# A macaron transformer block: 24 of 38 activation tiles are transposed by VectorE in 32x32 blocks and rearranged through HBM

## The chip, the cores and the metric

The kernel runs on one core of a Trainium2 chip. The metric is the device time of one execution in microseconds (us), the median of several runs. A core has five engines that each work through their own queue in order and wait for one another by semaphores: TensorE (PE in the profile, PEld for its weight loads), VectorE (DVE), ScalarE (ACT), GpSimd (POOL) and SyncE (SP). The last three here also issue DMA transfers. Tiles lie in SBUF, 128 partitions wide; TensorE writes to PSUM.

## The reference

All in float32: 256 tokens, width 2048, one block.

```python
h = rms_norm(x, ffn1_norm[i])
x = x + 0.5 * swiglu_ffn(h, ffn1_w_gate[i], ffn1_w_up[i], ffn1_w_down[i])   # D_FF = 5632
h = rms_norm(x, mix_norm[i])
proj = h @ w_in[i]
...
y_a = s5_mixer(u_a, ...)          # a state-space scan, then a GLU of 1024 x 1024
y_b = sgu_mixer(uv_b, ...)        # a gated mixing of tokens
gates = jax.nn.sigmoid(h @ w_gate[i] + b_gate[i])
g_a, g_b = jnp.split(gates, 2, axis=-1)
merged = g_a * (y_a @ w_branch_a[i]) + g_b * (y_b @ w_branch_b[i])
x = x + merged @ w_out[i]
h = rms_norm(x, ffn2_norm[i])
x = x + 0.5 * swiglu_ffn(h, ffn2_w_gate[i], ffn2_w_up[i], ffn2_w_down[i])
...
return rms_norm(x, final_norm)
```

where `swiglu_ffn(h, g, u, d)` is `(silu(h @ g) * (h @ u)) @ d`.

## The kernel before

**Weights.** All weight matrices stream from HBM once, in chunks of 128x2048 floats (1 MB), in the order of use. SP loads a chunk into `raw`; `split_piece` (L148, L149) makes of it a rounded high part `whi` on ScalarE and the remainder `wlo` on VectorE. Each product is then three matmuls (L216 to L218): high by high, high by low, low by high.

**Steps.** `take` hands out a chunk in four pieces of 512 columns, and every piece is a *step*: six matmuls, three for each half of the tokens. At the start of a step `tick` runs, in this order: the hooks that are due, the evacuation of the job that just ended (`pend`), at every fourth step the split of the chunk two ahead of the one in use (three buffers of `whi` and `wlo`), and a slice of side work when there is credit for it. What `tick` emits stands in that order in each engine's queue, so the program's text sets the order of everything.

**Jobs.** A `job` is one output tile of 256 tokens x 512 columns: `kt` steps into one PSUM accumulator `acc` (three buffers), then its evacuation. `at(n, fn)` puts `fn` into the hooks of the step that is n later.

**Transposes.** TensorE contracts over partitions, so a result that is the next product's input has to be transposed. `turned` does so 2 steps after the evacuation: eight 128x128 transposes on TensorE (L258) into two PSUM tiles `q`, then `put`, which splits `q` into high and low part on ScalarE and VectorE (`split2`: L244, L245; `split_gain` with a norm's gain: L248, L249). There are 38 such tiles:

- the feed-forward blocks, 11 each: the gated hidden tile, in groups of 4, 4 and 3 (`GROUPS`). `gate_evac` (L319) applies silu, `up_evac` (L329) multiplies, and `put` writes to `gt`. After a group come four jobs of the down product;
- *the first residual*, 4: after the first block's last down product (jobs of 12 steps) `residual` adds to `x_sb` (L294), squares for the norm, and the columns of `x_sb` are transposed into the next `h`;
- the mixers, 4;
- *the merge*, 4: `ba_evac` (L1026, L1027, jobs of 8 steps) combines the two branches, into `mT`;
- *the residual after w_out*, 4: the same `residual`, jobs of 16 steps.

**Side work.** In the first feed-forward block `s5_prepare` computes the scan's tables, 0.3 to 0.35 slices a step, with transfers through HBM that GpSimd issues (`stash_e`, `stash_v`, `stash_c`, `stash_g`, `stash_t`, `stash_w`; `eb`, `bt`, `par`, `tt` are loads). Five slices lie between the load of `eb` and `bt` and their use.

Of the kernel before, what the change touches and what calls it, by code (L numbers as in the profile page):

```python
# [9 lines left out]
F32 = mybir.dt.float32  # L10
F32R = mybir.dt.float32r
BF16 = mybir.dt.bfloat16
AF = mybir.ActivationFunctionType
ALU = mybir.AluOpType
# [4 lines left out]
P = 128  # L19
D = 2048  # L20
T = 256
DFF = 5632
KD = D // P
KF = DFF // P
EPS = 1e-6
N = 512
# [19 lines left out]
def f(ap):  # L46
    return ap.bitcast(F32)
# [3 lines left out]
def kernel(  # L51
# [31 lines left out]
    act, dve, pe, pool = nc.scalar, nc.vector, nc.tensor, nc.gpsimd  # L83

    cst = ctx.enter_context(tc.tile_pool(name="cst", bufs=1))
    ev = ctx.enter_context(tc.tile_pool(name="ev", bufs=1))
    wp = ctx.enter_context(tc.tile_pool(name="wp", bufs=1))
    hp = ctx.enter_context(tc.tile_pool(name="hp", bufs=1))
    dr = ctx.enter_context(tc.tile_pool(name="dr", bufs=1, space=DRAM))
# [4 lines left out]
    x_sb = cst.tile([P, 2, D], F32, name="x_sb")  # L94
# [72 lines left out]
    def at(delta, fn):  # L167
        hooks.setdefault(st["tick"] + delta, []).append(fn)
# [40 lines left out]
    def new_acc():  # L209
        return ps.tile([P, 2, N], F32, tag="acc", name="acc")  # L210

    def step(acc, lhs, k, first, last):
        hi, lo = take(N)
        for h in range(2):
            t = slice(h * P, h * P + P)
            pe.matmul(acc[:, h, :], lhsT=lhs[:, k, 0, t], rhs=hi, start=first, stop=False)  # L216
            pe.matmul(acc[:, h, :], lhsT=lhs[:, k, 0, t], rhs=lo, start=False, stop=False)  # L217
            pe.matmul(acc[:, h, :], lhsT=lhs[:, k, 1, t], rhs=hi, start=False, stop=last)  # L218

    def job(lhs, kt, evac):  # L220
        acc = new_acc()
        for k in range(kt):
            step(acc, lhs, k, k == 0, k == kt - 1)
        pend.append(lambda: evac(acc))
# [12 lines left out]
    def tmp():  # L237
        return ev.tile([P, 2, N], F32, tag="t", name="t", bufs=2)
# [1 line left out]
    def small():  # L240
        return ev.tile([P, 8], F32, tag="sm", name="sm", bufs=2)

    def split2(dst, src):
        act.activation(out=dst[:, :, 0, :], in_=src, func=AF.Copy)  # L244
        dve.tensor_tensor(out=dst[:, :, 1, :], in0=src, in1=f(dst[:, :, 0, :]), op=ALU.subtract)  # L245

    def split_gain(dst, src, g, k):
        act.activation(out=dst[:, 0, :], in_=src, func=AF.Copy, scale=g[:, k:k + 1])  # L248
        dve.scalar_tensor_tensor(out=dst[:, 1, :], in0=src, scalar=g[:, k:k + 1],  # L249
                                 in1=f(dst[:, 0, :]), op0=ALU.mult, op1=ALU.subtract)  # L250

    def turned(src, c0, put):
        for b in range(2):
            q = ms.tile([P, 2, T], F32, tag="ms", name="q")
            for i in range(2):
                for h in range(2):
                    c = c0 + (2 * b + i) * P
                    pe.transpose(q[:, i, h * P:h * P + P], src[:, h, c:c + P], ident)  # L258
            put(b, q)

    def rsqrt(dst, q, n, scratch):
        act.activation(out=dst, in_=q, func=AF.Sqrt, scale=1.0 / n, bias=eps_t)
        dve.reciprocal(dst, dst)
        dve.scalar_tensor_tensor(out=scratch, in0=q, scalar=EPS * n, in1=dst,
                                 op0=ALU.add, op1=ALU.mult)
        dve.scalar_tensor_tensor(out=scratch, in0=scratch, scalar=-0.5 / n, in1=dst,
                                 op0=ALU.mult, op1=ALU.mult)
        dve.scalar_tensor_tensor(out=dst, in0=scratch, scalar=1.5, in1=dst,
                                 op0=ALU.add, op1=ALU.mult)

    def square(m, h):
        j = ev.tile([P, N], BF16, tag="junk", name="junk", bufs=1)
        act.activation(out=j, in_=x_sb[:, h, m * N:m * N + N], func=AF.Square,  # L273
                       accum_out=ssq[:, h, m:m + 1])
# [14 lines left out]
    def rc(h):  # L289
        return norm["r"][:, h:h + 1]  # L290

    def add_residual(acc, m, scale):
        xs = x_sb[:, :, m * N:m * N + N]
        dve.scalar_tensor_tensor(out=xs, in0=acc, scalar=scale, in1=xs, op0=ALU.mult, op1=ALU.add)  # L294

    def residual(hT, g, scale):
        def make(m):
            def put(b, q):
                for i in range(2):
                    k = 4 * m + 2 * b + i  # L300
                    split_gain(hT[:, k], q[:, i, :], g, k)

            def evac(acc):
                add_residual(acc, m, scale)
                for h in range(2):
                    square(m, h)
                at(2, lambda: turned(x_sb, m * N, put))
                if m == 3:
                    at(4, new_norm)
            return evac  # L310
        return make

    def ffn(hT, gp, last_down, begin=None, rates=None):
        state = {}

        def gate_evac(acc):
            s = tmp()
            for h in range(2):
                act.activation(out=s[:, h, :], in_=acc[:, h, :], func=AF.Silu, scale=rc(h))  # L319
            state["g"] = s  # L320

        def up_evac(gt, j):
            def put(b, q):
                split2(gt[:, 4 * j + 2 * b:4 * j + 2 * b + 2], q)

            def evac(acc):
                s = state["g"]
                for h in range(2):
                    dve.scalar_tensor_tensor(out=s[:, h, :], in0=acc[:, h, :], scalar=rc(h), in1=s[:, h, :],  # L329
                                             op0=ALU.mult, op1=ALU.mult)  # L330
                at(2, lambda: turned(s, 0, put))
            return evac

        def down(m):
            return lambda acc: add_residual(acc, m, 0.5)

        for i, n in enumerate(GROUPS):
            gt = gp.tile([P, 16, 2, T], F32R, tag="gt", name="gt")
            if rates:
                credit[1] = rates[i]  # L340
            for j in range(n):
                if begin is not None and i == 0 and j == 0:
                    begin(gate_evac, up_evac(gt, j))
                    continue
                job(hT, KD, gate_evac)
                job(hT, KD, up_evac(gt, j))
            if i == len(GROUPS) - 1:
                last_down(gt, 4 * n)
            else:
                for m in range(4):  # L350
                    job(gt, 4 * n, down(m))
# [420 lines left out]
    def split_h1(k0):  # L772
        for k in (k0, k0 + 1):
            split_gain(h1[:, k], xT[:, k, :], g1, k)

    def begin(ev_g, ev_u):
        acc_g, acc_u = new_acc(), new_acc()
        for k in range(KD):
            for acc in (acc_g, acc_u):
                step(acc, h1, k, k == 0, k == KD - 1)  # L780
        pend.append(lambda: ev_g(acc_g))
        pend.append(lambda: ev_u(acc_u))
# [3 lines left out]
    for i, s in enumerate(pieces):  # L786
        if i < 2:
            split_gain(h1[:, i], xT[:, i, :], g1, i)
        split_piece(hi0, lo0, r0, s)
# [22 lines left out]
    def down_mix(gt, kt):  # L812
# [4 lines left out]
        for m in range(4):  # L817
            job(gt, kt, mk(m))

    ffn(h1, gp, down_mix, begin, (0.3, 0.35, 0.35))  # L820
    gp.release()
    h2 = box2["h"]
# [56 lines left out]
    def sgu():  # L879
        for c in range(2):  # L880
            for n in range(2):
                q = ms.tile([P, 4, P], F32, tag="ms", name="q")
                for i in range(4):
                    hd_ = 4 * c + i
                    pe.matmul(q[:, i, :], lhsT=ws_sb[:, hd_, :], rhs=v[:, n, hd_ * P:hd_ * P + P],  # L885
                              start=True, stop=True)
                yield
                for i in range(4):
                    hd_ = 4 * c + i
                    u = ub[:, n, hd_ * P:hd_ * P + P]  # L890
                    dve.scalar_tensor_tensor(out=u, in0=q[:, i, :], scalar=bs_sb[:, hd_:hd_ + 1], in1=u,
                                             op0=ALU.add, op1=ALU.mult)
            yield
            yield
            yield
            yield
            turned(ub, c * N, lambda b, q, c=c: split2(ybT[:, 4 * c + 2 * b:4 * c + 2 * b + 2], q))
            yield
# [58 lines left out]
    def cols(t, n):  # L957
        return t[:, :, n * N:n * N + N]
# [61 lines left out]
    def ba_evac(n):  # L1020
        def put(b, q):
            split2(mT[:, 4 * n + 2 * b:4 * n + 2 * b + 2], q)

        def evac(acc):
            t = tmp()
            dve.tensor_tensor(out=t, in0=acc, in1=cols(ga, n), op=ALU.mult)  # L1026
            dve.tensor_tensor(out=t, in0=t, in1=cols(mb, n), op=ALU.add)  # L1027
            at(2, lambda: turned(t, 0, put))
        return evac

    for n in range(4):
# [148 lines left out]
```

## Time and profile before

| | us |
|---|---|
| median of 3 runs (2053.28 to 2055.16) | 2055.1 |
| the profiled execution | 2053.59 |
| its span, from the first to the last instruction | 2051.8 |
| busy: TensorE | 2027.8 |
| busy: VectorE | 1127.6 |
| busy: ScalarE | 865.0 |
| busy: GpSimd | 72.8 |

The mean granted TensorE clock was 0.995 of full speed. The bytes moved came to 412 MB, a mean of 201 GB/s. In the profile a row of a group names the line, the engine, the operation, output<-input with shapes, the count, then the busy time in us with the mean duration in ns, then the idle time of the engine just before and what ended it. Matmuls are pipelined: one that lasts 0.39 us can start 0.23 us after the one before.

### The profile page before, as it was taken

The numbers are of one execution on the slowest core, as the hardware profiler recorded it, in microseconds if no ns is written. First come the engines' busy times: TensorE is split into PE (matmuls) and PEld (weight loads), VectorE is DVE, ScalarE is ACT, GpSimd is POOL, SyncE is SP. The second block draws the span as 40 slices with busy tenths as digits, with TensorE's granted clock in tenths as the row PEclk, the third lists the DMA queues.
The fourth block names the chain that finished last, engine by engine and source line by source line (L and its number), as shares of the span: only waits on it lengthen the run. The fifth ranks groups of instructions, "written<-read, shape, count | busy, mean of one in ns | idle before, by whom it ended". The sixth has DMA issues, their size and how long they took to land.

```text
span 2051.8 us, 23150 instructions
## 1 busy us (share of the span) xinstructions
PE 2027.8 (99%) x9764; PEld 1676.7 (82%) x9764; DVE 1127.6 (55%) x1102; ACT 865.0 (42%) x705; POOL 72.8 (4%) x134
## 2 busy tenths in 40 slices
PE   9999999999999999989999999999999999999997
PEld 7888888888888888878888888888888888888886
DVE  5765565555664555546765665544444444444454
ACT  6543334444334454434435444533433443333343
POOL 0000000111000000011100000000000000000000
PEclk9999999999999999999999999999999999999999
DMA  7557665565665455557765455555555555555552
GB/s 310 198 195 226 231 240 209 196 216 204 209 208 192 174 195 198 213 178 247 236 227 210 175 185 188 210 187 186 193 196 185 190 188 197 186 200 188 185 190 98
DMA packets 66489, 412.20 MB, mean 201 GB/s; under 512 B 10272, under 2 KB 10928, under 8 KB 20560
## 3 DMA queue, kind: packets, MB, share of 16 engines
q1 hardware_dynamic: 53280, 378.56, 52.0%
q0 software_dynamic: 10656, 27.93, 4.3%
q10 hardware_dynamic: 2448, 4.22, 0.6%
q8 instruction: 76, 1.25, 0.2%
q14 instruction: 29, 0.24, 0.0%
HBM read 398.21 MB, written 12.45 MB: 200 GB/s over the span
## 4 chain that ended last, share of the span: by engine, by line
PE 97%; DVE 1%; ACT 1%; issue 1%; DMA 0%; SPq 0%; ACTq 0%
PE acc L216 31%; PE acc L218 30%; PE acc L217 30%; PE q L258 2%; ACT whi L148 1%; PE q L588 0%; PE q L724 0%; PE acc L234 0%; PE acc L233 0%; PE acc L232 0%; DMA raw<-in_w1s_dram 0%; DVE wlo L149 0%; PE q L681 0%; PE q L885 0%; PE q L721 0%
## 5 line engine op out<-in xcount | busy, mean ns | idle before, releaser
L149 DVE TENSOR_TENSOR wlo<-raw,whi 128x2048 fp32r<-128x2048 f32 (+1 forms) x359 | 815.7, 2274 | 810.2 <-ACT whi L148 810.0
L148 ACT ACTIVATE whi<-raw 128x2048 fp32r<-128x2048 f32 (+1 forms) x359 | 682.2, 1901 | 913.2 <-PE acc L218 835.0
L216 PE MATMUL acc<-whi,h 128*128 128x512 f32 x1856 | 728.0, 392 | 1.2 <-ACT whi L148 1.2
L217 PE MATMUL acc<-wlo,h 128*128 128x512 f32 x1856 | 723.8, 390 | 2.2 <-DVE wlo L149 2.0
L218 PE MATMUL acc<-whi,h 128*128 128x512 f32 x1856 | 723.4, 390 | 0.0
L217 PEld LDWEIGHTS acc<-wlo,h 128*128 128x128 f32 x1856 | 349.2, 188 | 74.3 <-DVE wlo L149 3.2
L216 PEld LDWEIGHTS acc<-whi,h 128*128 128x128 f32 x1856 | 349.1, 188 | 74.2 <-ACT whi L148 1.6
L218 PEld LDWEIGHTS acc<-whi,h 128*128 128x128 f32 x1856 | 349.1, 188 | 73.0
L216 PE MATMUL acc<-whi,gt 128*128 128x512 f32 x680 | 266.1, 391 | 0.0
L218 PE MATMUL acc<-whi,gt 128*128 128x512 f32 x680 | 266.1, 391 | 0.0
L217 PE MATMUL acc<-wlo,gt 128*128 128x512 f32 x680 | 265.1, 390 | 0.0
L217 PEld LDWEIGHTS acc<-wlo,gt 128*128 128x128 f32 x680 | 127.7, 188 | 27.6
L218 PEld LDWEIGHTS acc<-whi,gt 128*128 128x128 f32 x680 | 127.7, 188 | 27.1
L216 PEld LDWEIGHTS acc<-whi,gt 128*128 128x128 f32 x680 | 127.7, 188 | 26.6
L319 ACT ACTIVATE t<-acc,rc 128x512 f32<-128x512 f32 x44 | 27.9, 686 | 63.4 <-PE acc L218 63.4
L216 PE MATMUL acc<-whi,mT 128*128 128x512 f32 x128 | 50.2, 392 | 0.0
L294 DVE SCALAR_TENSOR_TENSOR x_sb<-acc,x_sb 128x1024 f32<-128x1024 f32 x27 | 33.1, 1225 | 30.9 <-PE acc L218 30.9
L218 PE MATMUL acc<-whi,mT 128*128 128x512 f32 x128 | 49.9, 389 | 0.0
L217 PE MATMUL acc<-wlo,mT 128*128 128x512 f32 x128 | 49.8, 389 | 0.0
L273 ACT ACTIVATE junk<-x_sb 128x512 bf16<-128x512 f32 x32 | 20.2, 631 | 66.2 <-DVE x_sb L294 53.0
L329 DVE SCALAR_TENSOR_TENSOR t<-acc,rc,t 128x512 f32<-128x512 f32 x44 | 31.0, 745 | 16.8 <-PE acc L218 16.8
L244 ACT ACTIVATE gt<-q 128x512 fp32r<-128x512 f32 x44 | 23.9, 596 | 29.1 <-PE q L258 29.1
(200 smaller groups left out, 1067.3 us busy)
## 6 DMA issues: line engine op xcount, KB each, us to landing
raw<-in_w1d_dram SPq DMA_DIRECT2D x44, 1024.0 KB, 4.9
raw<-in_w2g_dram SPq DMA_DIRECT2D x44, 1024.0 KB, 4.8
raw<-in_w2u_dram SPq DMA_DIRECT2D x44, 1024.0 KB, 4.8
raw<-in_w2d_dram SPq DMA_DIRECT2D x44, 1024.0 KB, 4.8
raw<-in_w1g_dram SPq DMA_DIRECT2D x40, 1024.0 KB, 4.8
raw<-in_w1u_dram SPq DMA_DIRECT2D x40, 1024.0 KB, 4.9
raw<-in_w_in_dram SPq DMA_DIRECT2D x24, 1024.0 KB, 4.8
raw<-in_w_gb_dram SPq DMA_DIRECT2D x16, 1024.0 KB, 5.3
```

What stands on the lines that cost most here:

```text
L148: act.activation(out=hi[:, s], in_=r[:, s], func=AF.Copy)
L149: dve.tensor_tensor(out=lo[:, s], in0=r[:, s], in1=f(hi[:, s]), op=ALU.subtract)
L216: pe.matmul(acc[:, h, :], lhsT=lhs[:, k, 0, t], rhs=hi, start=first, stop=False)
L217: pe.matmul(acc[:, h, :], lhsT=lhs[:, k, 0, t], rhs=lo, start=False, stop=False)
L218: pe.matmul(acc[:, h, :], lhsT=lhs[:, k, 1, t], rhs=hi, start=False, stop=last)
L244: act.activation(out=dst[:, :, 0, :], in_=src, func=AF.Copy)
L258: pe.transpose(q[:, i, h * P:h * P + P], src[:, h, c:c + P], ident)
L273: act.activation(out=j, in_=x_sb[:, h, m * N:m * N + N], func=AF.Square, accum_out=ssq[:, h, m:m + 1])
L294: dve.scalar_tensor_tensor(out=xs, in0=acc, scalar=scale, in1=xs, op0=ALU.mult, op1=ALU.add)
L319: act.activation(out=s[:, h, :], in_=acc[:, h, :], func=AF.Silu, scale=rc(h))
L329: dve.scalar_tensor_tensor(out=s[:, h, :], in0=acc[:, h, :], scalar=rc(h), in1=s[:, h, :], op0=ALU.mult, op1=ALU.mult)
```

## The change

For 24 of the 38 tiles `turned` is replaced by `turned_dma`: in the feed-forward blocks all but the last tile of each group (3, 3 and 2 of 4, 4 and 3, twice: 16), in both residuals the first three of four (6), in the merge the first two of four (2). At the evacuation itself VectorE transposes the 32x32 blocks of the tile, once for each half of the tokens, into a second tile `t`. GpSimd writes that to a buffer `turn` in HBM (two of them), 512 KB in rows of 4 KB, and reads it back in 16 transfers of 32 KB into two tiles `w`, in runs of 32 floats, so that the blocks come to lie where a whole transpose has them. `w` shares its two buffers with the `bias` tiles. `put` then reads `w` instead of `q`; it runs a fixed number of steps after the evacuation (18 in the feed-forward blocks, 15 in the residuals, 14 in the merge) instead of 2.

```diff
+    def turned_dma(src, c0, put, wait):
+        tt = tmp()
+        for h in range(2):
+            dve.transpose(out=tt[:, h, :], in_=src[:, h, c0:c0 + N])
+        d = dr.tile([P, 2, N], F32, tag="turn", name="turn", bufs=2)
+        pool.dma_start(out=d, in_=tt)
+        dv = d.rearrange("(a j) h (k b i) -> k a b j h i", a=4, b=4, k=4)
+        ws = []
+        for b in range(2):
+            w = ev.tile([P, 2, T], F32, tag="bias", name="w", bufs=2)
+            for i in range(2):
+                for a in range(4):
+                    pool.dma_start(out=w[:, i].rearrange("p (h a i) -> p a h i", h=2, a=4)[:, a],
+                                   in_=dv[2 * b + i, a])
+            ws.append(w)
+
+        def arrived():
+            for b in range(2):
+                put(b, ws[b])
+        at(wait, arrived)
...
-                at(2, lambda: turned(x_sb, m * N, put))
+                if m < 3:
+                    turned_dma(x_sb, m * N, put, 15)
+                else:
+                    at(2, lambda: turned(x_sb, m * N, put))
...
-                at(2, lambda: turned(s, 0, put))
+                if j < n - 1:
+                    turned_dma(s, 0, put, 18)
+                else:
+                    at(2, lambda: turned(s, 0, put))
...
-            at(2, lambda: turned(t, 0, put))
+            if n < 2:
+                turned_dma(t, 0, put, 14)
+            else:
+                at(2, lambda: turned(t, 0, put))
```

GpSimd's queue at the start of the first feed-forward block, before (`lc` and `lm` are s5_prepare's first loads; what stands in brackets are the semaphores waited for, DMASW0 to DMASW7 those of GpSimd's own transfers):

```order
L372 DMA lc<-in_s5l_dram 128x96 [waits DMAHW4_49,DMAHW3_49,DMAHW7_49,DMAHW1_49,DVE_49]
L373 DMA lm<-in_s5m_dram 64x192
L491 DMA stash_e<-em 32x4x64 [waits DVE_49] x2
L491 DMA stash_e<-em 32x4x64 x2
L542 DMA eb<-stash_e 128x1x512 [waits DMASW2_49,DMASW3_49,DMASW1_49,DMASW5_49,DVE_49,Activation_49]
```

and now, the second tile's write and the first of its reads:

```order
L268 DMA turn<-t 128x1024 [waits DMASW4_49,DVE_49]
L275 DMA w<-turn 128x2x32 [waits DMASW5_49,DMASW4_49,Activation_49]
L275 DMA w<-turn 128x2x32 [waits DMASW6_49]
L275 DMA w<-turn 128x2x32 [waits DMASW7_49]
L275 DMA w<-turn 128x2x32 [waits DMASW0_49]
L275 DMA w<-turn 128x2x32 [waits DMASW1_49]
L275 DMA w<-turn 128x2x32 [waits DMASW2_49]
L275 DMA w<-turn 128x2x32 [waits DMASW3_49]
```

Three tiles' transfers now stand ahead of the first load of `eb`; a tile's first read waits for its write and for the splits that read the `w` of the tile before, and each transfer for the one eight before it, so that eight are in flight at most.

VectorE's queue in the merge, before (`mT<-q` is the split of a transposed tile, `t<-acc,ga` and `t<-t,mb` the evacuation, `wlo` the split of a weight chunk):

```order
L1026 TENSOR_TENSOR t<-acc,ga 128x1024
L1027 TENSOR_TENSOR t<-t,mb 128x1024
L149 TENSOR_TENSOR wlo<-raw,whi 128x2048
L245 TENSOR_TENSOR mT<-q,mT 128x2x256 x2
L149 TENSOR_TENSOR wlo<-raw,whi 128x2048
```

and now, from the split of tile 0 on:

```order
L247 TENSOR_TENSOR mT<-w,mT 128x2x256 x2
L1055 TENSOR_TENSOR t<-acc,ga 128x1024
L1056 TENSOR_TENSOR t<-t,mb 128x1024
L149 TENSOR_TENSOR wlo<-raw,whi 128x2048
L247 TENSOR_TENSOR mT<-q,mT 128x2x256 x2
L149 TENSOR_TENSOR wlo<-raw,whi 128x2048
L247 TENSOR_TENSOR mT<-w,mT 128x2x256 x2
L1055 TENSOR_TENSOR t<-acc,ga 128x1024
L1056 TENSOR_TENSOR t<-t,mb 128x1024
```

The split of tile 0 stands ahead of tile 2's evacuation and that of tile 1 ahead of tile 3's; before, each tile's split came two steps after its own evacuation.

VectorE's queue in the residual after w_out, before:

```order
L294 SCALAR_TENSOR_TENSOR x_sb<-acc,x_sb 128x2x512
L149 TENSOR_TENSOR wlo<-raw,whi 128x2048
L249 SCALAR_TENSOR_TENSOR h_8622<-q,vec_sb,h_8622 128x256 x4
L149 TENSOR_TENSOR wlo<-raw,whi 128x2048 x3
L294 SCALAR_TENSOR_TENSOR x_sb<-acc,x_sb 128x2x512
```

and now:

```order
L317 SCALAR_TENSOR_TENSOR x_sb<-acc,x_sb 128x2x512
L266 STREAM_TRANSPOSE t<-x_sb 128x512 x2
L149 TENSOR_TENSOR wlo<-raw,whi 128x2048 x4
L251 SCALAR_TENSOR_TENSOR h_8791<-w,vec_sb,h_8791 128x256 x4
L317 SCALAR_TENSOR_TENSOR x_sb<-acc,x_sb 128x2x512
```

The split into `h` now stands directly ahead of the next tile's evacuation, with no weight split between.

More of the change, by code (lines that the diff above doesn't have):

```diff
@@ L241, in small, with split2, split_gain @@
         return ev.tile([P, 8], F32, tag="sm", name="sm", bufs=2)
[L243 to L250, printed above, removed]
+    ALL = slice(0, T)
+    def split2(dst, src, c=ALL):
+        act.activation(out=dst[:, :, 0, c], in_=src, func=AF.Copy)
+        dve.tensor_tensor(out=dst[:, :, 1, c], in0=src, in1=f(dst[:, :, 0, c]), op=ALU.subtract)
+    def split_gain(dst, src, g, k, c=ALL):
+        act.activation(out=dst[:, 0, c], in_=src, func=AF.Copy, scale=g[:, k:k + 1])
+        dve.scalar_tensor_tensor(out=dst[:, 1, c], in0=src, scalar=g[:, k:k + 1],
+                                 in1=f(dst[:, 0, c]), op0=ALU.mult, op1=ALU.subtract)
     def turned(src, c0, put):
@@ L320, in gate_evac, with up_evac @@
             state["g"] = s
-        def up_evac(gt, j):
+        def up_evac(gt, j, n):
             def put(b, q):
@@ L342, in ffn @@
                 if begin is not None and i == 0 and j == 0:
-                    begin(gate_evac, up_evac(gt, j))
+                    begin(gate_evac, up_evac(gt, j, n))
                     continue
                 job(hT, KD, gate_evac)
-                job(hT, KD, up_evac(gt, j))
+                job(hT, KD, up_evac(gt, j, n))
             if i == len(GROUPS) - 1:
```

## The prediction, made before the changed kernel had run

> **What bounds the kernel now.** I read the page first: busy times, then the chain of waits.
>
> ```profile
> PE 2027.8 (99%) x9764; PEld 1676.7 (82%) x9764; DVE 1127.6 (55%) x1102; ACT 865.0 (42%) x705; POOL 72.8 (4%) x134
> PE 97%; DVE 1%; ACT 1%; issue 1%; DMA 0%; SPq 0%; ACTq 0%
> PE acc L216 31%; PE acc L218 30%; PE acc L217 30%; PE q L258 2%; ACT whi L148 1%; PE q L588 0%; PE q L724 0%; PE acc L234 0%; PE acc L233 0%; PE acc L232 0%; DMA raw<-in_w1s_dram 0%; DVE wlo L149 0%; PE q L681 0%; PE q L885 0%; PE q L721 0%
> ```
>
> TensorE is on the ending chain for 97% of the span. The transposes (L258) hold 2% of it; VectorE is idle 45% of the time, GpSimd 96%. So an instruction taken off TensorE is a gain in full, as long as TensorE then waits for nobody new. Next, TensorE's timeline around one transposed tile in the last feed-forward stage (start, duration, then the instruction; the gap between starts is the real pace, since matmuls overlap):
>
> ```profile
> 1350.75 0.39 PE L217 MATMUL acc<-wlo,h 128*128 128x512 f32 x1
> ...
> 1355.05 0.40 PE L218 MATMUL acc<-whi,h 128*128 128x512 f32 x1
> 1355.29 1.04 PE L258 MATMUL q<-ident,t 128*128 128x128 f32 x8
> 1356.08 0.47 PE L216 MATMUL acc<-whi,h 128*128 128x512 f32 x1
> ...
> 1359.61 0.39 PE L216 MATMUL acc<-whi,h 128*128 128x512 f32 x1
> ```
>
> From 1350.75 to 1355.05 lie 19 starts, 0.227 us each; a step of six matmuls is 1.36 us. From 1355.05 to 1359.61 lie 16 starts that would need 3.63 us and take 4.56: **a tile's eight transposes cost TensorE 0.93 us**. The last view says how long ScalarE and VectorE may be held up before TensorE notices: the splits of one weight chunk (four steps).
>
> ```profile
> 1297.45 1.92 ACT L148 ACTIVATE whi<-raw 128x2048 fp32r<-128x2048 f32 x1 [0.80 <-PE acc L218]
> 1302.93 1.92 ACT L148 ACTIVATE whi<-raw 128x2048 fp32r<-128x2048 f32 x1 [3.57 <-PE acc L218]
> 1299.40 2.29 DVE L149 TENSOR_TENSOR wlo<-raw,whi 128x2048 fp32r<-128x2048 f32 x1 [0.42 <-ACT whi L148]
> ```
>
> A chunk is split when TensorE releases a buffer, every 5.5 us, and is used two chunks (eight steps, 10.9 us) later. The two splits take 4.2 us, so they may start 6.7 us late.
>
> **The change part by part.** *Removed:* of 304 transposes, 38 tiles of eight (kind, count, duration min/median/max in ns):
>
> ```profile
> L258 PE MATMUL q<-ident,t x224: 270/272/447, 57.9 to 1974.6; 128*128 128x128 f32 x112
> L258 PE MATMUL q<-ident,x_sb x64: 270/272/273, 706.8 to 1311.6; 128*128 128x128 f32 x64
> L258 PE MATMUL q<-ident,ub x16: 270/272/273, 863.6 to 895.9; 128*128 128x128 f32 x16
> ```
>
> The median barely differs between the kinds, so every tile is taken at the price read above: 24 x 0.93 = **22.3 us** of TensorE.
>
> *Added on VectorE:* two 32x32-block transposes of 128x512 for each tile. The trace has no such operation. Bounds: 0.48 us (256 columns) and 1.23 us (1024 columns).
>
> ```profile
> L249 DVE SCALAR_TENSOR_TENSOR h<-q,vec_sb,h 128x256 fp32r<-128x256 f32 x32 | 14.7, 480 | 8.7 <-ACT h L248 8.7
> L381 DVE TENSOR_TENSOR m<-eb,bt 128x512 f32<-128x512 f32 x16 | 10.6, 687 | 0.1
> L294 DVE SCALAR_TENSOR_TENSOR x_sb<-acc,x_sb 128x1024 f32<-128x1024 f32 x27 | 33.1, 1225 | 30.9 <-PE acc L218 30.9
> L245 DVE TENSOR_TENSOR mT<-q,mT 128x512 fp32r<-128x512 f32 x8 | 5.1, 683 | 0.0
> L244 ACT ACTIVATE mT<-q 128x512 fp32r<-128x512 f32 x8 | 4.3, 596 | 5.4 <-PE q L258 5.4
> ```
>
> I take 0.69 us, the SBUF-to-SBUF operation of the same shape: 1.4 us a tile, 33 us in all, covered by VectorE's idle 45%. The splits that read `w` instead of PSUM (L245, L244) I leave at their 0.68 and 0.60 us.
>
> *Added on GpSimd's queue:* 24 x 17 transfers, one 512 KB write and 16 reads of 32 KB with 256 runs of 128 bytes. What bears on their price:
>
> ```profile
> 356.37 4.23 POOL L600 DMA_DIRECT2D tt<-stash_g  x8 [1.71 <-issue]
> 362.71 0.58 POOL L601 DMA_DIRECT2D stash_t<-tt  x1 [2.11 <-DMA tt<-stash_g]
> L544 POOL DMA_DIRECT2D bt<-in_s5bt_dram x4: 749/764/769, 157.3 to 268.7; - x4
> L914 POOL DMA_DIRECT2D u_dr<-u_all x4: 712/718/745, 876.5 to 910.6; - x4
> stash_v<-vt POOLq DMA_DIRECT2D x4, 512.0 KB, 5.0
> tt<-stash_g POOLq DMA_DIRECT2D x8, 32.0 KB, 3.5
> u<-u_dr POOLq DMA_DIRECT2D x8, 128.0 KB, 7.3
> q1 hardware_dynamic: 53280, 378.56, 52.0%
> q0 software_dynamic: 10656, 27.93, 4.3%
> ```
>
> `tt<-stash_g` is the nearest kin, a read back from HBM in 128 short runs: 4.23/8 = 0.53 us to issue, 3.5 us to land. `bt` writes two runs into each of 128 partitions, just as a read of `w` does: 0.76 us. So a read costs between 0.53 and, if the price goes with the runs, 2 x 0.53 = 1.06 us of GpSimd's queue. I take 0.76 for the count of runs that it shares. For landing I take 3.5 us (end: 7.3, `u`), and 5.0 for the write. From the end of its transposes a tile then needs 5.0 + 15 x 0.76 + 3.5 = **19.9 us**. The bytes do little: 25 MB more is about what q0 moves now in 4.3% of the engines' time, next to weights that take 52%.
>
> The Trainium skill, "DMA: Bandwidth & Descriptors", section "Why a DMA increments its semaphore by 16 and not by 1", says that a transfer is spread over at most as many engines as divide the slowest dimension of both sides; that is four for `w`, whose HBM side begins with a dimension of 4. The trace cannot show it for `w`; q1's mean packet (52.0% of 16 x 2051.8 us is 17,071 us, for 53,280 packets: 0.32 us for 7.1 KB) makes 8 KB on each of four engines some 0.3 us longer to land, an estimate, and the sum below 1.5 us worse over five tiles.
>
> *Feed-forward, 16 tiles.* Two gated multiplies (0.74 us each), the transposes, 19.9: the tile is in SBUF 22.8 us after its job ends. Its splits stand at step 18, between the chunk splits of steps 16 and 20. The latter must begin by 38.1 - 4.2 = 33.9 us. Hidden with 10 us to spare, until a read costs 1.4 us. In the first block s5_prepare's own transfers are queued behind a tile's reads and come up to 16 x 0.76 = 12 us later. The tightest are these (KB each, median us to landing):
>
> ```profile
> eb<-stash_e POOLq DMA_DIRECT2D x8, 256.0 KB, 8.6
> ```
>
> 12 + 8.6 us is still inside the five slices (0.3 a step: 17 steps, 22.7 us) that the code leaves between load and use, so I cost it at nothing. Without that cover VectorE would wait at `eb` for those 12 us, 5 us more than its splits can be late.
>
> *First residual, 3 tiles*, 12 steps (16.3 us) apart. Each tile's write is queued on GpSimd behind the 16 reads of the one before. Tile 0 lands at 1.2 + 1.4 + 19.9 = 22.5 us, tile 1 (write at 19.9) at 39.8, tile 2 (write at 37.1) at 57.0; with 1.5 us of splits (ScalarE 0.47, then VectorE twice 0.48) each is before its limit (28.4, 44.8, 61.2). Nothing.
>
> *The merge, 2 tiles*, 8 steps (10.9 us) apart.
>
> ```profile
> 1193.51 1.23 DVE L1026 TENSOR_TENSOR t<-acc,ga 128x1024 f32<-128x1024 f32 x1 [1.36 <-PE acc L218]
> 1194.77 1.23 DVE L1027 TENSOR_TENSOR t<-t,mb 128x1024 f32<-128x1024 f32 x1
> ```
>
> By the order of the program, tile 0's split stands on VectorE ahead of tile 2's evacuation, which TensorE's transposes of tile 2 need at step 18 (24.5 us). Tile 0 lands at 2.5 + 1.4 + 19.9 = 23.8, is split at 25.1, tile 2 is evacuated at 27.6: **TensorE waits 3.1 us**. Tile 1's write waits for tile 0's reads (21.1), lands at 41.0, is split at 42.3; tile 3 is evacuated behind it at 44.8, where its transposes stand at step 26, now 38.5: **6.3 us**.
>
> *Residual after w_out, 3 tiles*, 16 steps (21.8 us) apart. The split of a tile (step 15) stands on VectorE ahead of the next evacuation (step 16). A tile takes 22.5 + 1.5 = 24.0 us, so each puts the next 2.2 us later; the fourth is evacuated 6.6 us late (plus 1.2) while its transposes stand two steps (2.7) behind: **5.1 us**.
>
> The sum: -22.3 + 3.1 + 6.3 + 5.1 = **-7.8 us**. The profiled execution took 2053.6 us (span 2051.8), 1.5 below the median of 2055.1: that is 2046 on its own scale, and **2047** against the median.
>
> **The rivals.** *All hidden:* reads at 0.53 us. A tile needs 5.0 + 8.0 + 3.5 = 16.5 us; w_out's chain falls to 20.6, under 21.8, and in the merge only tile 3 waits, 2.2 us. -20 us: 2035. `tt` speaks for it, `bt` and `u_dr` (0.72) against.
>
> *Slower: the reads set the pace of the merge and of both residuals.* At 1.06 us a tile needs 24.4 us. w_out: 28.6 against 21.8, three times, 19 us; the merge 7.6 + 11.1; the first residual 5.7 + 5.6. 49 us lost, 22.3 won: +27, 2082. Landing at 7.3 us comes to much the same, since the program lets only eight GpSimd transfers be in flight (7.3/8 = 0.91 us a read, the last 7.3 later). Between 14.5 us lost at 0.76 and 49 at 1.06 it turns at 0.83 us a read. `u` speaks for it, but at four times the bytes; a read with a four-index source is shown nowhere.
>
> *Much slower: every run of 128 bytes costs a packet.* At q1's 0.32 us, 4096 runs on 16 engines are 82 us a tile; the feed-forward tiles would land some 60 us past their limit: 16 x 60, about +960 us, near 3000. Against it stand eight `tt` reads, 1024 runs, all landed 6.3 us after the first issue, where this price asks 20. The Trainium skill, "VectorE: DVE Perf Modes", section "The three transpose paths", warns that a plain copy that transposes by strides is 19 times slower than the crossbar's when the innermost destination stride is large. Here the innermost stride is one element for 32, so by the `tt` rows the warning does not carry over.
>
> **How the numbers follow.** The forecast case (2039 to 2053) gets 0.43, all hidden (2030 to 2039) 0.16, the slower rival 0.36 (2053 upward, most of it under 2080), the packet price 0.05. The range 2032 to 2078 leaves out the packet price, the far end of the slower rival and the best corner, 0.2 together. A measurement tells about 0.2% (4.1 us) from no change: faster is below 2051, which is all hidden and most of the forecast, 0.53; within 0.2% (2051 to 2059) 0.15, from where the two meet; slower 0.32.
>
> **What would show it.** TensorE: 112 transposes instead of 304, the weight matmuls' pace still 0.227 us. VectorE: transposes of about 0.69 us. GpSimd: reads of `w` at 0.76 us, landing in 3.5. In the feed-forward stages ScalarE must not wait for the reads of `w` longer than a few us, and TensorE not at all. Around the merge TensorE should wait at the transposes of `t` and, at the end of w_out, at those of `x_sb`, 15 us together. The prediction is wrong if a read costs over 0.83 us or under 0.6, if TensorE waits for `whi` in the feed-forward stages, or if loads of weights get late.

## The result, and the profile after

| us | before | after |
|---|---|---|
| median of four runs | 2054.5 | 2154.0 |
| lowest to highest | 2053.3 to 2055.2 | 2145.6 to 2160.4 |
| the profiled execution | 2053.6 | 2145.6 |
| its span | 2051.8 | 2143.8 |

The changed kernel is slower: ratio 1.048, 95% interval [1.045, 1.051]. I forecast 2047 in a range of 2032 to 2078. The page after begins with the busy times; the granted clock over 40 slices (in tenths of full speed) and the two large DMA queues stand further down:

```profile
PE 2035.4 (95%) x9572; PEld 1670.4 (78%) x9572; DVE 1157.6 (54%) x1150; ACT 863.7 (40%) x705; POOL 597.5 (28%) x542
PEclk9999999999999989999999979889999999999999
q1 hardware_dynamic: 53280, 378.56, 51.0%
q0 software_dynamic: 32544, 54.30, 12.8%
```

The clock row of the page before was:

```profile
PEclk9999999999999999999999999999999999999999
```

192 matmuls are gone, and still TensorE is busy for longer in a span that grew by 92.0 us. GpSimd went from 73 us to 598. At three places the clock of a slice falls under nine tenths, which no slice did before. What GpSimd does is seen in the rows of the two new lines (kind, count, duration min/median/max in ns) and in their transfers' landing times; last comes the transpose on VectorE:

```profile
L275 POOL DMA_DIRECT2D w<-turn x384: 1328/1334/1402, 62.0 to 2044.7; - x192
L268 POOL DMA_DIRECT2D turn<-t x24: 533/577/603, 58.2 to 2020.1; - x24
w<-turn POOLq DMA_DIRECT2D x384, 32.0 KB, 6.5
turn<-t POOLq DMA_DIRECT2D x24, 512.0 KB, 3.6
L266 DVE STREAM_TRANSPOSE t<-t x36: 660/682/712, 56.6 to 2019.1; 128x512 f32<-128x512 f32 x36
```

**A read holds GpSimd for 1.334 us, not 0.76, and lands after 6.5 us, not 3.5.** The write is cheaper than taken (3.6), the block transpose as taken (0.68). From the end of its transposes a tile needs 3.6 + 15 x 1.334 + 6.5 = 30.1 us where I had 19.9.

What TensorE waited for (total us, times, longest):

```profile
PE acc L217 <- DVE wlo L149: 25.4, 19, 1.8
PE acc L216 <- ACT whi L148: 24.1, 9, 6.8
PE q L260 <- DVE t L1056: 22.0, 2, 11.6
PE q L260 <- DVE x_sb L317: 11.8, 1, 11.8
```

None of these rows names a transfer. The releasers are the weight splits, the merge's evacuation and the residual's, and what stands ahead of those is the split of a tile that hasn't arrived (ScalarE's waits):

```profile
ACT gt L246 <- DMA w<-turn: 103.0, 15, 9.9
ACT h L250 <- DMA w<-turn: 72.0, 22, 6.8
ACT mT L246 <- DMA w<-turn: 25.6, 4, 9.6
```

The merge shows it in order of time, GpSimd first, then VectorE:

```profile
1222.83 21.33 POOL L275 DMA_DIRECT2D w<-turn  x16 [2.63 <-DMA turn<-t]
1244.15 0.59 POOL L268 DMA_DIRECT2D turn<-t  x1
...
1247.41 0.69 DVE L247 TENSOR_TENSOR mT<-w,mT 128x512 fp32r<-128x512 f32 x1 [6.63 <-ACT mT L246]
1248.02 1.22 DVE L1055 TENSOR_TENSOR t<-acc,ga 128x1024 f32<-128x1024 f32 x1
1249.27 1.23 DVE L1056 TENSOR_TENSOR t<-t,mb 128x1024 f32<-128x1024 f32 x1
```

Sixteen reads hold GpSimd for 21.3 us. The tile's last split on VectorE comes at 1247.41, tile 2's evacuation right behind it, and TensorE's transposes of tile 2 start at 1250.56, after a wait of 10.4 us. Tile 1, evacuated 11 us after tile 0, gets its write out at 1244.15, when tile 0's last read is issued.

The feed-forward stages have less of it. One tile of the second block, on GpSimd, VectorE, ScalarE and TensorE:

```profile
1490.87 0.58 POOL L268 DMA_DIRECT2D turn<-t  x1 [18.20 <-DVE t L266]
...
1487.94 1.41 DVE L355 SCALAR_TENSOR_TENSOR t<-acc,rc,t 128x512 f32<-128x512 f32 x2 [1.22 <-PE acc L218]
...
1522.17 0.63 ACT L246 ACTIVATE gt<-w 128x512 fp32r<-128x512 f32 x1 [8.88 <-DMA w<-turn]
1522.70 5.50 ACT L148 ACTIVATE whi<-raw 128x2048 fp32r<-128x2048 f32 x3
...
1526.99 0.50 PE L217 MATMUL acc<-wlo,h 128*128 128x512 f32 x1 [0.78 <-DVE wlo L149]
```

The job ends at 1487.9, its tile has arrived 34.2 us later, and three chunk splits that had queued up run back to back. By the prediction's limit of 33.9 us the first had to begin at 1521.8; it begins 0.9 us late, and TensorE waits 0.8 us.

From the starts of all matmuls in the two traces the 92 us divide so: 22 us of transposes fewer; gaps of over 1 us between starts, 88 us more (18 in the feed-forward blocks, 18 at the first residual, 22 in the merge, 29 at the residual after w_out); 14 us because 88 weight matmuls, where it was 16 before, start 0.427 us after the one before instead of 0.227, nearly all of them behind such gaps; some 8 us of shorter gaps; about 4 us not placed.

### The profile page after: what moved, and what is told of

It is laid out like the page before. It is cut to its first block, busy times and chain, and to the rows that moved or that the text cites. A ratio compares the mean times of both kernels' runs of the same rounds, so it can differ in the third digit from the quotient of the medians.

```text
span 2143.8 us, 23665 instructions
## 1 busy us (share of the span) xinstructions
PE 2035.4 (95%) x9572; PEld 1670.4 (78%) x9572; DVE 1157.6 (54%) x1150; ACT 863.7 (40%) x705; POOL 597.5 (28%) x542
## 5 line engine op out<-in xcount | busy, mean ns | idle before, releaser
L216 PE MATMUL acc<-whi,h 128*128 128x512 f32 x1856 | 731.7, 394 | 13.4 <-ACT whi L148 10.4
L275 POOL DMA_DIRECT2D w<-turn x384 | 510.8, 1336 | 87.1 <-issue 39.0
L216 PEld LDWEIGHTS acc<-whi,h 128*128 128x128 f32 x1856 | 351.4, 189 | 91.2 <-ACT whi L148 13.3
L268 POOL DMA_DIRECT2D turn<-t x24 | 13.8, 574 | 756.9 <-DVE t L266 756.8
L217 PEld LDWEIGHTS acc<-wlo,gt 128*128 128x128 f32 x680 | 128.1, 188 | 30.1 <-DVE wlo L149 2.1
L247 DVE TENSOR_TENSOR gt<-w,gt 128x512 fp32r<-128x512 f32 x32 | 22.1, 689 | 120.9 <-ACT gt L246 118.1
L246 ACT ACTIVATE gt<-w 128x512 fp32r<-128x512 f32 x32 | 20.2, 630 | 149.3 <-DMA w<-turn 103.0
L216 PE MATMUL acc<-whi,mT 128*128 128x512 f32 x128 | 53.0, 414 | 12.3 <-ACT whi L148 12.3
L218 PE MATMUL acc<-whi,mT 128*128 128x512 f32 x128 | 52.2, 408 | 0.0
```

The costliest lines, as they stand in the source:

```text
L246: act.activation(out=dst[:, :, 0, c], in_=src, func=AF.Copy)
L247: dve.tensor_tensor(out=dst[:, :, 1, c], in0=src, in1=f(dst[:, :, 0, c]), op=ALU.subtract)
L268: pool.dma_start(out=d, in_=tt)
L275: pool.dma_start(out=w[:, i].rearrange("p (h a i) -> p a h i", h=2, a=4)[:, a], in_=dv[2 * b + i, a])
```

## The experiments

**1 and 2. The feed-forward tiles alone, and the same with a later split.** Both keep the change in the feed-forward blocks only (16 tiles).

```diff
-                if m < 3:
+                if m < 0:
...
-            if n < 2:
+            if n < 0:
```

The second also splits eight steps later:

```diff
-                    turned_dma(s, 0, put, 18)
+                    turned_dma(s, 0, put, 26)
```

The first, expected:

> Only the 16 feed-forward tiles go through HBM, the 8 of the residuals and the merge stay on TensorE. Theory A (the reads' issue time of 1.33 us on GpSimd makes the tiles late, and what costs is the splits that stand in the queues in front of other work): the 8 tiles of the residuals and the merge carry nearly all of the loss, because only there is the time between a tile's evacuation and its split too short; by the changed kernel's matmul starts the feed-forward blocks alone lose some 15 us net, so 2069, range 2055 to 2080. Theory B (the short runs crowd the 16 DMA engines and the weights come late): the loss goes with the number of tiles, 16/24 of the 122 us lost, less 15 won: 2121.

The second, expected:

> As the run before, with the splits of the feed-forward tiles 26 steps after the evacuation instead of 18; the transfers are the same. Theory A: a tile lands 34 us after its job, the limit moves from 33 to 44 us, no split is late, and the 16 x 0.93 us of TensorE are won: 2040, range 2036 to 2046. Theory B: the transfers are the same, so is the loss: the same time as the run before, within 5 us.

Measured: 2065.8 us, ratio 1.0056 [1.0038, 1.0073], and 2042.0 us, ratio 0.9934 [0.9918, 0.9951]. ScalarE's groups at the split of `w`, of the first and of the second (count, busy us and mean ns, then idle before and its releasers):

```profile
L246 ACT ACTIVATE gt<-w 128x512 fp32r<-128x512 f32 x32 | 20.2, 630 | 152.0 <-DMA w<-turn 102.4 <-DMA stash_c<-ca 16.6 <-issue 14.6
```

```profile
L246 ACT ACTIVATE gt<-w 128x512 fp32r<-128x512 f32 x32 | 18.3, 615 | 2.5 <-issue 1.8 <-DMA w<-turn 0.7
```

The transfers are the same in both; one number in the program takes the wait away, and with it 24 us. So the feed-forward loss is a split that stands 18 steps behind its evacuation for data that needs 25 steps, in front of a weight split. With the later split TensorE has no new wait in the feed-forward blocks, though the DMA traffic and GpSimd's time are the same. Outside of them run 2 has one: 3.7 us in the mixers for `tab`, a table that GpSimd loads; what made that load late isn't shown. I had named the limit ("until a read costs 1.4 us"); 1.33 with the longer landing has reached it.

**3. The rearrangement in the write instead of the read.** All 24 tiles. Four writes of 128 KB lay the 32x32 blocks where a whole transpose has them, in runs of 128 bytes; two plain reads of 256 KB bring the tile back.

```diff
-        d = dr.tile([P, 2, N], F32, tag="turn", name="turn", bufs=2)
-        pool.dma_start(out=d, in_=tt)
-        dv = d.rearrange("(a j) h (k b i) -> k a b j h i", a=4, b=4, k=4)
+        d = dr.tile([4, P, 2, P], F32, tag="turn", name="turn", bufs=2)
+        dv = d.rearrange("k (b j) h (a i) -> a j h (k b) i", b=4, a=4)
+        for a in range(4):
+            pool.dma_start(out=dv[a], in_=tt[32 * a:32 * a + 32].rearrange("j h (c i) -> j h c i", i=32))
...
-            for i in range(2):
-                for a in range(4):
-                    pool.dma_start(out=w[:, i].rearrange("p (h a i) -> p a h i", h=2, a=4)[:, a],
-                                   in_=dv[2 * b + i, a])
+            pool.dma_start(out=w, in_=d[2 * b:2 * b + 2].rearrange("k p h c -> p k (h c)"))
```

> All 24 tiles; the rearrangement is in the write (4 transfers of 128 KB in runs of 128 bytes, all 16 engines) and the read back is 2 transfers in runs of 1 KB. As many short runs as in the changed kernel, 6 transfers a tile instead of 17. Theory A with a price by the runs that one engine gets (64 for a write here as for a read there: 1.33 us): 4 x 1.33 + 2 x 0.76 = 6.8 us of GpSimd a tile, landing some 16 us after the transposes, feed-forward and residuals hidden, a few us lost in the merge: 2036, range 2031 to 2046. Price by runs in all (1024 a write, four times 1.33): 23 us of GpSimd a tile, about 2150 as now. Theory B: the short runs are the same, so about 2150.

Measured: **2032.5 us, ratio 0.9894 [0.9880, 0.9909]**, faster than both kernels. Its page, the rows of the two lines, and their landing:

```profile
PE 2005.2 (99%) x9572; PEld 1657.5 (82%) x9572; DVE 1154.1 (57%) x1150; ACT 864.2 (43%) x705; POOL 185.2 (9%) x278
...
L270 POOL DMA_DIRECT2D turn<-t x96: 814/818/857, 58.5 to 1910.5; - x96
L274 POOL DMA_DIRECT2D w<-turn x48: 713/718/728, 68.9 to 1921.3; - x48
...
turn<-t POOLq DMA_DIRECT2D x96, 128.0 KB, 5.1
w<-turn POOLq DMA_DIRECT2D x48, 256.0 KB, 4.6
```

A tile holds GpSimd for 4 x 0.82 + 2 x 0.72 = 4.7 us instead of 21.9, and 22 us are gained, the whole price of 192 transposes. The tiles, the bytes, the count of short runs and the places of the splits are the same: so the loss is not in moving transposes through HBM, but in the form or the count of the transfers, which run 4 separates. The expected price of a write, 1.33 us, is a miss, though: it was 0.82. With four times as many runs as one of the changed kernel's reads it costs less than one, so neither "by runs" nor "by runs for each engine" is the law.

**4. Sixteen reads of another form.** The writes of run 3, but 16 reads with the destinations of the changed kernel; their source now begins with a dimension of 128 rows of 256 bytes instead of 4.

```diff
-                                   in_=dv[2 * b + i, a])
+                                   in_=d[a, 2 * b + i].rearrange("p (h i) -> p h i", h=2))
```

> All 24 tiles; 4 writes as in the run before into another layout, then 16 reads with the same destinations as in the changed kernel (two runs of 128 bytes in each of 128 partitions), but from rows of 256 bytes whose outermost dimension is 128, not 4. Price by runs for one engine (16 instead of 64): a read at 0.65 to 0.76 us, 12 us a tile plus 5.3 for the writes; late in the merge and the residuals still, near 2085. Price by runs in all (256, as in the changed kernel): a read at 1.33 us, over 26 us of GpSimd a tile, 2200 or more.

Measured: 2057.3 us, ratio 1.0015 [1.0003, 1.0028] (ten runs). The reads, their landing, and TensorE's longest waits:

```profile
L276 POOL DMA_DIRECT2D w<-turn x384: 702/710/726, 64.4 to 1953.7; - x192
w<-turn POOLq DMA_DIRECT2D x384, 32.0 KB, 4.5
...
PE q L260 <- DVE t L1057: 8.9, 2, 8.4
PE q L260 <- DVE x_sb L318: 7.2, 2, 6.7
```

The reads' count, bytes and destination are unchanged; the source's form halves the issue and takes 2 us off the landing, and 97 us of time go. Both expected times are too long. The first had the read's price right (0.65 to 0.76 expected, 0.71 measured) and the writes' too high (1.33 each, 0.82 measured); the second, 1.33 us by the count of runs, is refuted. The longest waits left, 16 us, are in the merge and at w_out, where I had forecast them: at 0.71 us a read, with four writes of 0.82 ahead, this is near the kernel that I predicted. It is still 10 us slower than 2047. By the starts of matmuls the gaps of over 1 us cost 20 us where the prediction had 14.5, and the half pace behind them costs 4 more.

**5, 6 and 7. One of the other three places at a time**: the first residual (3 tiles), the merge (2), the residual after w_out (3), each with the changed kernel's transfers and all else transposed on TensorE. The conditions:

```diff
-                if m < 3:
+                if m < 3 and scale == 0.5:    # first residual; scale == 1.0: after w_out; m < 0: merge alone
...
-                if j < n - 1:
+                if j < 0:
```

The first residual:

> Only the three tiles of the first residual go through HBM, as in the changed kernel. Theory A, the prediction's own working with the prices measured on the changed kernel (write landed after 3.6 us, a read 1.33 us to issue and 6.4 to land, so 30.0 us a tile, each write behind the 16 reads before it): the splits end 5.7, 8.5 and 8.5 us past their limits, 22.7 us, less 2.8 won: +20, 2074, up to 5 more if the clock drops after each wait. Theory B (crowded DMA engines): 3/24 of the loss of 100: 2067, and no wait of TensorE for whi or wlo.

The merge:

> Only the two tiles of the merge go through HBM. Theory A by the same working: TensorE waits 13.2 us at the transposes of tile 2 and 14.0 at those of tile 3, less 1.9 won: +25, 2080. Theory B: 2/24 of the loss of 100: 2063.

The residual after w_out:

> Only the three tiles of the residual after w_out go through HBM. Theory A by the same working: a tile takes 34.1 us where 21.8 are there, each puts the next 12.3 us later, 35.4 us at the end, less 2.8 won: +33, 2087, up to 7 more for the clock. Theory B: as the first residual, 2067. The three terms and the feed-forward run's +11 should sum to the changed kernel's +100 within 15 if nothing but these waits costs.

| | measured, us | ratio | lost, with the transposes saved | prediction's working at the measured prices |
|---|---|---|---|---|
| first residual | 2076.7 | 1.0106 [1.0090, 1.0121] | 22.4 + 2.8 = 25.2 | 22.8 |
| merge | 2077.2 | 1.0109 [1.0092, 1.0126] | 22.9 + 1.9 = 24.8 | 13.3 + 14.0 = 27.3 |
| after w_out | 2087.0 | 1.0156 [1.0141, 1.0171] | 32.6 + 2.8 = 35.4 | 3 x 12.4 + 1.2 - 2.7 = 35.7 |

The last column takes the sums of the prediction with 3.6, 1.334 and 6.5 us for write, read and landing. After w_out, for instance, a tile then takes 34.2 us instead of 24.0 where tiles come 21.8 us apart: three times 12.4. Each agrees to 3 us, but two errors nearly cancel in that. By the starts of matmuls in the three traces, the gaps of over 1 us came to 17, 24 and 28 us more than before, where the working has 23, 27 and 36; and starts at half pace behind them added 6, 2 and 5 us, which the working doesn't hold. After w_out TensorE's wait doesn't stand at the last transposes alone, as the prediction had it: 12.3 us do, and 12.5 stand at weight splits (`whi`) before. With run 1 (11.4 us above the kernel before) the four excesses make 89 us. The profiled execution of the changed kernel, the fastest of its four, is 92 us above the one before, and its median 99.5; what the other runs add isn't shown.

**8. The issue time by itself.** The kernel before, with eight loads of 32 KB in each of ten forms at an idle place of GpSimd's queue, and eight in the changed kernel's form on SP's; the loaded values are not used. A single run, 2055.6 us. Two of the forms (`l_after` is that of the changed kernel):

```diff
+        for s in slot("l_after"):
+            pool.dma_start(out=two(s), in_=turn[0, 0])
...
+        for s in slot("l_two"):
+            pool.dma_start(out=two(s), in_=flat[0:P * 128].rearrange("(p h x) -> p h x", p=P, h=2)[:, :, 0:32])
```

> The kernel before, with 80 reads of 32 KB from a weight in HBM into unused SBUF in the second feed-forward block, where GpSimd's queue is empty: eight each of ten shapes, and eight of the changed kernel's shape from SyncE's queue. The issue time of each shape is what is asked. If it goes with the DMA engines that a transfer is spread over (outermost dimension 2, 4, 8, 16, 32 of a source that can't be merged): 4 as in the changed kernel's 1.33 us, 16 and 32 near 0.71, 2 above 2. If it goes with the runs (128 or 256): the five with 128 runs alike, near 0.55. If it is the four-index source alone: only that shape is at 1.33. From SyncE's queue: 0.33 us as the weight loads if the queue's hardware makes the descriptors, over 1 us if its price goes with the runs too. The kernel's time says nothing here.

GpSimd's groups (count, busy us and mean ns, then idle before); the names leave numbers out, so the rows `l_c` are told apart by line. The fifth of these comes last, in another view (min/median/max in ns):

```profile
L1058 POOL DMA_DIRECT2D l_after<-in_w2g_dram x8 | 10.6, 1334 | 45.0 <-DVE t L953 45.0
L1076 POOL DMA_DIRECT2D l_c4two<-in_w2g_dram x8 | 10.6, 1332 | 0.7 <-DMA l_c16two<-in_w2g_dram 0.7
L1064 POOL DMA_DIRECT2D l_c<-in_w2g_dram x8 | 6.4, 833 | 5.0 <-DMA l_two<-in_w2g_dram 5.0
L1062 POOL DMA_DIRECT2D l_two<-in_w2g_dram x8 | 5.6, 711 | 4.2 <-DMA l_plain<-in_w2g_dram 4.2
L1074 POOL DMA_DIRECT2D l_c16two<-in_w2g_dram x8 | 5.4, 689 | 0.0
L1066 POOL DMA_DIRECT2D l_c<-in_w2g_dram x8 | 5.4, 678 | 8.9 <-DMA l_c<-in_w2g_dram 8.9
L1068 POOL DMA_DIRECT2D l_c<-in_w2g_dram x8 | 4.7, 622 | 6.6 <-DMA l_c<-in_w2g_dram 6.6
L1060 POOL DMA_DIRECT2D l_plain<-in_w2g_dram x8 | 4.3, 547 | 4.5 <-DMA l_after<-in_w2g_dram 4.5
L1070 POOL DMA_DIRECT2D l_c<-in_w2g_dram x8 | 4.2, 548 | 5.4 <-DMA l_c<-in_w2g_dram 5.2 <-issue 0.3
...
L1072 POOL DMA_DIRECT2D l_c<-in_w2g_dram x8: 564/594/642, 1207.5 to 1211.2; - x8
```

| first dimension of the source | 128 runs of 256 bytes | 256 runs of 128 bytes |
|---|---|---|
| 2 | 0.83 (L1064) | |
| 4 | 0.68 (L1066) | 1.33 (L1058, L1076) |
| 8 | 0.62 (L1068) | |
| 16 | 0.55 (L1070) | 0.69 (L1074) |
| 32 | 0.59 (L1072, median) | |
| 128 | 0.55 (L1060) | 0.71 (L1062) |

The changed kernel's form costs 1.33 us in an idle queue too, so its price doesn't come from other transfers of that queue. `l_c4two` has another four-index layout and the same price, `l_c16two` the same layout with 16 in front and half the price: the four-index source as such is cleared. Twice the runs cost double behind a first dimension of 4 and 26 to 30% more behind 16 or 128. A first dimension of 4 costs 24% more than 16 with 128 runs, and 93% more with 256. So each has a price alone, and together they cost more than the product: 0.55 x 1.24 x 1.26 would be 0.86 us, and 1.33 was measured. No theory with a single cause had that, and why it is so isn't shown. On SP's queue the form of `w` took 0.56 us (median; the longest of the eight 2.75).

**9 and 10. TensorE kept busy through the merge's waits.** Run 6 with matmuls of the identity ahead of the transposes of tiles 2 and 3, 100 and then 48; their result is overwritten.

```diff
+            for _ in range(fill if b == 0 else 0):
+                pe.matmul(q[:, 0, :P], lhsT=ident, rhs=ident, start=True, stop=True)
```

With 100, expected:

> The merge's two tiles through HBM, as in the run of them alone (2077.2), with 100 matmuls of 128x128 on the identity ahead of the transposes of tile 2 and of tile 3, into the PSUM tile that the transposes then overwrite: 10.7 us of TensorE at 0.107 us each, inside the waits of 12.2 and 11.5 us. If TensorE's idle time is what halves its pace afterwards: the transposes and the 12 slow starts of weight matmuls behind the two waits come at full pace, and the time falls by some 4 us (2.5 for the weight matmuls, twice 0.8 for the transposes): 2073. If something else slows them (the splits that come late, say), the slow starts stay and the time stays within 1.5 us of 2077.

With 48, expected:

> The run of the merge alone (2077.2 us) with 48 identity matmuls ahead of the transposes of tiles 2 and 3. Each is two recorded passes of 0.1125 us, so the fill is 96 x 0.1125 = 10.8 us a tile, against gaps of 12.2 and 11.5 us there without it. A (idling itself costs the half pace that followed each gap): the gaps are filled and the end of each wait doesn't move, so only the slow starts go away: 0.1 us for each of some 40 transposes and 0.2 for each of 12 weight matmuls less, 3 to 6 us, about 2073, and no weight matmul at half pace behind the gaps. B (the half pace belongs to what follows the wait, not to the idling): the slow starts stay, and the time is 2077.

Measured: 2098.1 us, ratio 1.0217 [1.0200, 1.0234], and 2077.9 us, ratio 1.0122 [1.0104, 1.0140]. One stretch in the window view of run 6 and of run 10 (length, then busy us of TensorE, its loads, VectorE, ScalarE, GpSimd; granted clock; DMA share; GB/s), and TensorE behind run 10's fills:

```profile
1200.00:1260.00 60.00, 36.60 (x151) 29.88 (x151) 22.79 (x19) 15.98 (x14) 34.08 (x27) 0.80 0.54 130
```

```profile
1200.00:1260.00 60.00, 56.43 (x347) 50.10 (x346) 23.46 (x18) 14.34 (x15) 32.46 (x26) 0.97 0.53 130
...
1217.99 1.09 PE L262 MATMUL q<-ident,t 128*128 128x128 f32 x8 [0.84 <-DVE t L1058]
1219.16 0.39 PE L217 MATMUL acc<-wlo,yas 128*128 128x512 f32 x1
1219.39 0.39 PE L218 MATMUL acc<-whi,yas 128*128 128x512 f32 x1
...
1243.50 1.09 PE L262 MATMUL q<-ident,t 128*128 128x128 f32 x8 [2.73 <-DVE t L1058]
1245.24 0.63 PE L218 MATMUL acc<-whi,mT 128*128 128x512 f32 x1
1245.67 0.63 PE L216 MATMUL acc<-whi,mT 128*128 128x512 f32 x1
```

The first fill was mis-sized: each of its matmuls is two passes of 0.1125 us, 22.5 us in gaps of 12, so that run says nothing on time; afterwards no weight matmul ran at half pace. With 48, 0.84 us of idling is left of the first gap and the matmuls behind it start 0.23 us apart; 2.73 us is left of the second, and behind the transposes eight weight matmuls start 0.43 us apart, as without a fill. So the half pace follows idling, and the clock column shows it (0.80 without the fill, 0.97 with it). But the time didn't move (I expected 3 to 6 us from it). By the traces run 10 had gained 1.9 us on run 6 behind the first gap; at the end of the second wait, which the reads' landing sets, it was 0.2 us behind, and the faster starts after it won 1.0. What the half pace costs behind the first gap of run 6 is thus hidden by the next wait.

## Why the prediction was wrong, step by step

- *The read's issue time* is the step that failed: 0.76 us taken, 0.53 to 1.06 as bounds, 1.334 measured. Of the 10.2 us by which a tile's transfers took longer than the 19.9 forecast, 8.6 are these 15 issues and 3.0 the landing; the write gave 1.4 back. I took it from `bt` by the count of runs in each partition and set the upper end by doubling `tt` for twice the runs. That doubling assumes one cause. Run 8 shows two that make each other dearer: 256 runs, and a source whose first dimension is 4. Runs 3 and 4, which change the form and keep the tiles, show that the loss goes with this price and the landing that comes with it: 2154 becomes 2032 or 2057.
- *Landing*: 3.5 taken, 6.5 measured, inside the bound of 7.3. The Trainium skill, "DMA: Bandwidth & Descriptors", section "Why a DMA increments its semaphore by 16 and not by 1", has a rule that bears on this: a transfer uses the largest number of engines, up to 16, that divides the first dimension of both sides, four here. I had charged that rule 0.3 us of landing only. The runs agree with its grouping: 4.5 us to land in run 4 against 6.5, and run 8's prices for 128 runs fall until the first dimension is 16 and no further (0.55, then 0.59 and 0.55). The page says nothing of an issue time that follows it.
- *The write* (5.0 taken, 3.6 measured), *the block transposes* (0.69, 0.68) and *24 x 0.93 us of TensorE* were right; run 3 shows the last, with 22 us gained.
- *Feed-forward, nothing, "until a read costs 1.4 us"*: the mechanism and the limit were right, the price reached it. Lost in run 1: 11.4 + 14.9 (16 tiles) = 26 us, of which run 2 gives back 24.
- *First residual, nothing; merge 9.4; w_out 5.1*: the places and what stands behind what were read rightly, and nearly all of the error is the price. Because each tile's write waits for the reads of the one before, it is paid per read, 16 times a tile. That the same sums at the measured prices meet runs 5 to 7 to 3 us is in part luck, since they put the waits 3 to 8 us too high and leave the half pace out.
- *The slower rival* had the mechanism, all three places, and +27 us. Its turning point of 0.83 us a read was passed; its price stopped at 1.06. Its chance of 0.36 was set by a bound that didn't bound: a form that "is shown nowhere" was costed as if the nearest row could only be doubled.
- *All hidden* is what run 3 gives (2032 against 2035), with other transfers, so that the number met is no proof of its price of 0.53 us a read. *A packet for each run* is out: run 3 moves as many runs of 128 bytes, and its writes land in 5.1 us.
- *Left out*: that TensorE runs at half pace after a wait, 14 us. The trace before had it: behind waits of 4.6 and 1.2 us from 872 us on weight matmuls start 0.43 us apart, and the clock from 868 to 888 us is 0.83.

## What to carry to other kernels

Price a DMA on GpSimd's queue by its form before its bytes: a small first dimension of the source and a high count of short runs make each other dearer, and a first dimension of 4 with 256 runs of 128 bytes was the dearest form measured here. Put the rearrangement on the side where few transfers do it, and keep the other side plain. When data comes back by transfer, what counts is what stands behind its first reader in that engine's queue, and moving that reader later (from 18 to 26 steps) won 24 us here without touching a transfer.

## What the runs showed of the hardware that I had not expected

**TensorE starts at half pace behind waits of a few us.** In the changed kernel's windows around the merge and w_out:

```profile
1220.00:1280.00 60.00, 38.03 (x159) 31.08 (x158) 28.61 (x23) 16.18 (x14) 43.38 (x34) 0.81 0.61 145
1280.00:1400.00 120.00, 92.81 (x381) 74.63 (x380) 48.30 (x37) 38.51 (x40) 65.53 (x51) 0.88 0.65 166
```

The half pace comes in stretches of 3 to 10 starts, most of them of six to eight: 8 x 0.427 = 3.4 us. The Trainium skill, "TensorE: Matmul & The Clock Gate", section "Part 1: The HAM clock gate", says that the clock is either full or half, and that it is granted by windows of about 3.4 us in which TensorE was busy or idle. The length of the stretches agrees. Less idling than the whole idle window of that page was enough here: 2.73 us in run 10, and a gap of 2.3 us between two starts at 415 us in the changed kernel. It isn't always enough: behind the same gap of 2.3 us at 2056 us no start is slow.

**SP issued the dear form at GpSimd's cheapest price**: a median of 0.56 us against 1.33 for the same access pattern (run 8), though the eight together held SP's queue for 7.3 us. No kernel was run with the reads on SP's queue, where they would stand between the weight loads.
